# One ring of 4 KB buffers for a decoder trunk's weights, late FFN features, q and k and pooled features, and each quad's first product placed ahead of the preceding quad's last

## The chip, the cores and the metric

The kernel runs on one core of a Trainium2 chip. The metric is the device time of one execution in microseconds (us); lower is better.

## The reference, cut to what matters

```python
D_MODEL, SEQ, DEPTH, D_FF = 1024, 512, 2, 2816      # float32 throughout

def swiglu(x, w_gu, w_down):
    g, u = jnp.split(x @ w_gu, 2, axis=-1)
    return (jax.nn.silu(g) * u) @ w_down

for i in range(DEPTH):                              # mixer 0: attention, 1: pooling
    x = layer_norm(ALPHA * x + 0.5 * swiglu(x, ffn_w_gu[i, 0], ffn_w_down[i, 0]), ...)
    x = layer_norm(ALPHA * x + mixer_i(x), ...)
    x = layer_norm(ALPHA * x + 0.5 * swiglu(x, ffn_w_gu[i, 1], ffn_w_down[i, 1]), ...)
```

Six stages follow one another on 512 tokens of 1024 channels: FFN, attention (8 heads, T5 bias), FFN, FFN, pooling mixer (four groups with a causal mean each), FFN. Each ends in a LayerNorm, and the next stage needs its result.

## The kernel before, in words

**Phases.** The profile's span divides into FFN 0 (0 to 363 us), attention (363 to 588), FFN 2 (588 to 932), FFN 3 (932 to 1278), pooling (1278 to 1382) and FFN 5 (1382 to 1736).

**Precision.** Every float32 operand is split in two (`split`, L94): ScalarE copies it to fp32r (L96, `hi`), VectorE subtracts that from it (L97, `lo`). A product is three matmuls (`mm3`, L101 to L103).

**Weights.** They stream from memory in pieces of 512 KB (4 KB in each partition). SyncE issues the loads (L183), in the order in which the pieces are used; where a sum of two pieces is wanted, GpSimd adds the second by an accumulating DMA (L185). The pieces lie in a ring `raw` of 7 buffers. A weight *unit* is a piece, or a sum of pieces made by two adds on VectorE (`Quad.sums`, L139), split to `hi` and `lo`, each in a ring of 5. `run_ahead` keeps 5 units split ahead of TensorE, called from `retire` whenever a unit has been used; `load_ahead` loads a piece once the piece seven before it has been used up.

**FFN.** The first block has four plain units, done for the first half of the tokens (`h=0`) and then for the second (`h=1`). The second half's first operand, x8, is what `Seven.put` splits from the last token tiles. Between the halves, `x.sums()` forms the sums of x that the quads need (`form`, L279, then a split). Then come ten *quads*: Strassen's scheme with seven products, in the order 1, 2, 6, 5, 7, 3, 4, each one unit of 24 matmuls of 256 columns. Products are kept by ScalarE (L504) or added by VectorE (`ca`, `cb`, L507); the gate writes the FFN's features to `hT` (L512), 22 blocks of 2 KB. Products 1, 6, 7 and 4 accumulate one after the other in one bank; `cb` reads it after product 7, so product 4 waits for that add. After that come the down projection, residual and LayerNorm (L344 to L367), and transposes to feature-major order (L312, then L323 on ScalarE or L321 on VectorE), of which the last token tiles' come in the next phase.

**Order.** TensorE's order is that of the program. VectorE, ScalarE, GpSimd and SyncE run what a scheduler set at build time, in order on each engine. Buffers with one tag are given out as they are free.

Of the kernel before, what the change touches and what calls it, by code (L numbers as in the profile page):

```python
# [79 lines left out]
def trunk(ctx, tc, x, rel_bias, ln_g, ln_b, w_gu, w_dq, w_down, a_in, a_out, b_in, b_group, b_scale, b_out, onehot, out):  # L80
# [67 lines left out]

    def ffn_units(l, m):
        for i in range(4):  # L150
            plain(w_gu[l, m, 0, i])
        for jj in QUADS:
            q = Quad(w_gu[l, m, jj])
            for i in LATER:
                q.unit(i)
        both = [Quad(w_dq[l, m, q]) for q in range(2)]
        pieces[-10:] = [q.pieces[i] for group in ((0,), (1,), (2,), (3,), (4,)) for q in both for i in group]
        for i in LATER:
            for q in both:
                q.unit(i)  # L160
        b_plain(w_down[l, m], range(BLOCK, NF))
# [25 lines left out]

    def load_ahead():
        while len(loaded) < len(pieces) and (len(loaded) < RAW or pieces[len(loaded) - RAW].uses == 0):
            load()  # L190

    def prepare():
# [3 lines left out]
        hi = wp.tile([P, 1024], F32R, tag="hi", bufs=PARTS, name=f"hi{i}")  # L196
        lo = wp.tile([P, 1024], F32R, tag="lo", bufs=PARTS, name=f"lo{i}")
# [275 lines left out]
    def bias_rows(room):  # L473

        oh, gs, rb = room[0:BUCKETS, 0:GW], room[0:H, 1024:1024 + GW], room[0:BUCKETS, 2048:2048 + H]
        nc.gpsimd.dma_start(oh, onehot)
        nc.gpsimd.dma_start(rb, rel_bias)
        gp = bank(6, "gp")
        nc.tensor.matmul(gp[:H, :], rb, oh[:, 0:512], start=True, stop=True)
# [14 lines left out]
    def ffn(n, x, dest):  # L494
        with tc.tile_pool(name=f"ffn{n}", bufs=1) as fp:
            hT = fp.tile([P, NF, S], F32, name=f"hT{n}")
            kept = {}
# [50 lines left out]
            for jj in QUADS:  # L548
                if n == 0 and jj == 2:
# [1 line left out]
                if n == 0 and jj == 4:
                    bias_rows(hT[:, 14:22, :].rearrange("p f c -> p (f c)"))
                if jj == 2:
# [1 line left out]
                ca = fp.tile([P, 2, S], F32, tag="ca", name=f"ca{n}_{jj}")
                cb = fp.tile([P, 2, 256], F32, tag="cb", name=f"cb{n}_{jj}")
                banks = [bank(i, f"gu{n}_{jj}_{i}") for i in (2 * ((jj + 1) % 3), 2 * ((jj + 1) % 3) + 1, 6 + jj % 2)]
                for i in LATER:
                    acc = banks[BANKS[i]]
                    for _ in product([acc[:, 0:256], acc[:, 256:512]], weights(), x.parts[i], i in (1, 2, 5), i in (2, 3, 4)):  # L560
                        pass
                    if i in (1, 6):
                        keep(i, jj, acc, 2)
                    elif i == 5:
                        keep(i, jj, acc, 1)
                    elif i == 2:
                        add(ca[:, :, 0:256], acc, 1, jj)
                    elif i == 3:
                        add(ca[:, :, 256:512], acc, 6, jj)
                        ins = gate(2 * jj, 0, 512, ca[:, 0, :], ca[:, 1, :], 1.0)  # L570
                        if 3 <= jj < 3 + NT:
                            update_residual(ins)
                    elif i == 7:
                        add(cb, acc, 5, jj)
                        gate(2 * jj + 1, 256, 512, cb[:, 0, :], cb[:, 1, :], -1.0)
                    else:
                        gate(2 * jj + 1, 0, 256, acc[:, 0:256], acc[:, 256:512], -1.0)
                    retire()
                    if jj == QUADS[-1] and i in (2, 6, 3):
                        next(operands)  # L580
# [43 lines left out]
    def attention(n, x, dest):  # L624
        with tc.tile_pool(name="att", bufs=1) as ap:
            oT, qk, v, probs, pT = {}, {}, {}, {}, {}

            def project(acc, nm, h):
                two = [ap.tile([P, S], F32R, tag=f"{nm}{i}", bufs=2, name=f"{nm}{i}_{h}") for i in range(2)]
                split(two[0], two[1], acc)  # L630
                qk[nm, h] = two
# [111 lines left out]
    def pooling(n, x, dest):  # L743
        with tc.tile_pool(name="pool", bufs=1) as pp:
# [7 lines left out]
            def pool(acc, cc):  # L752
# [131 lines left out]
```

## Time and profile before

| | |
|---|---|
| runs | 1738.93 us median of 3 (1737.85 to 1741.2) |
| profiled execution | 1737.85 us, span 1736.1 us |
| TensorE | 1705.0 us busy (98%), mean granted clock 0.997 |
| VectorE | 1251.3 us (72%) |
| ScalarE | 825.6 us (48%) |
| GpSimd | 94.5 us (5%) |
| DMA | 257.30 MB, mean 148 GB/s |
| chain that ended last | TensorE 93%, DMA 3%, VectorE 2%, issue 1% |

The busy figures are shares of the whole span. A matmul's end is modelled and matmuls overlap, so the space between matmuls is read from their starts. A wait at one place need not show in the shares; it shows in the list of waits and in windows of time.

### The profile page before, as it was taken

What the parts mean: (1) busy time and instruction counts of PE and PEld (TensorE: products, weight loads), DVE (VectorE), ACT (ScalarE), POOL (GpSimd) and SP (SyncE); (2) the same over time, 40 slices, a digit from 0 to 9 for tenths busy, and PEclk for the clock granted to TensorE, in tenths of its full rate; (3) what the DMA queues carried; (4) which work ended last, traced back from release to release, by engine and by line L of the source; (5) the groups of instructions that cost most, each with busy time, mean ns of one, the idle gap of its engine ahead of it and who ended that gap; (6) DMA issues with size and microseconds to landing.
All of it is one profiled execution on the core that took longest, in us unless ns stands there. A gap on an engine that the chain in (4) does not pass through costs nothing.

```text
span 1736.1 us, 28083 instructions
## 1 busy us (share of the span) xinstructions
PE 1705.0 (98%) x11555; PEld 1585.1 (91%) x11555; DVE 1251.3 (72%) x1657; ACT 825.6 (48%) x1161; POOL 94.5 (5%) x132
## 2 busy tenths in 40 slices
PE   7999999999999999999999999999999999999998
PEld 6999998889888899999888999998888899999886
DVE  5777698266665877878928778788279787877946
ACT  5545464254443555455525554564254454545620
POOL 1010000000000000000000000000000000000000
PEclk9999999999999999999999999999999999999999
DMA  6787756323221376666633666756223356776611
GB/s 209 188 238 186 189 146 209 97 74 110 86 86 51 109 194 176 185 181 164 194 97 85 183 182 185 184 154 197 96 88 106 99 166 187 185 189 180 185 62 49
DMA packets 84864, 257.30 MB, mean 148 GB/s; under 512 B 8128, under 2 KB 25576, under 8 KB 84736
## 3 DMA queue, kind: packets, MB, share of 16 engines
q1 hardware_dynamic: 70080, 202.40, 35.0%
q0 software_dynamic: 14656, 53.12, 17.1%
q8 instruction: 90, 1.47, 0.3%
q14 instruction: 38, 0.31, 0.1%
HBM read 253.37 MB, written 4.74 MB: 149 GB/s over the span
## 4 chain that ended last, share of the span: by engine, by line
PE 93%; DMA 3%; DVE 2%; issue 1%; ACT 0%; SPq 0%; DVEq 0%; POOLq 0%
PE gu L101 16%; PE gu L102 16%; PE gu L103 16%; PE acc L102 8%; PE acc L103 8%; PE acc L101 8%; DMA raw<-in_ffn_w_gu 2%; PE qk L103 2%; PE da L102 2%; PE da L101 2%; PE da L103 2%; PE qk L101 2%; PE qk L102 2%; PE d L102 1%; PE d L103 1%; PE d L101 1%
## 5 line engine op out<-in xcount | busy, mean ns | idle before, releaser
L96 ACT ACTIVATE hi<-raw 128x1024 fp32r<-128x1024 f32 x458 | 484.6, 1061 | 661.4 <-PE gu L102 251.8
L97 DVE TENSOR_TENSOR lo<-raw,hi 128x1024 fp32r<-128x1024 f32 x458 | 557.5, 1222 | 323.6 <-ACT hi L96 322.0
L101 PE MATMUL gu<-x,hi 128*128 128x256 f32 x2496 | 710.3, 285 | 12.4 <-DVE x L97 6.7
L102 PE MATMUL gu<-x,hi 128*128 128x256 f32 x2496 | 707.8, 284 | 0.0
L103 PE MATMUL gu<-x,lo 128*128 128x256 f32 x2496 | 707.7, 284 | 0.0
L101 PEld LDWEIGHTS gu<-x,hi 128*128 128x128 f32 x2496 | 480.7, 193 | 16.6 <-DVE x L97 9.7
L102 PEld LDWEIGHTS gu<-x,hi 128*128 128x128 f32 x2496 | 480.8, 193 | 0.0
L103 PEld LDWEIGHTS gu<-x,lo 128*128 128x128 f32 x2496 | 480.6, 193 | 0.0
L101 PE MATMUL acc<-lo,h 128*128 128x512 f32 x448 | 174.8, 390 | 0.0
L103 PE MATMUL acc<-hi,h 128*128 128x512 f32 x448 | 174.3, 389 | 0.0
L102 PE MATMUL acc<-hi,h 128*128 128x512 f32 x448 | 174.3, 389 | 0.0
L139 DVE TENSOR_TENSOR raw<-raw,raw 128x1024 f32<-128x1024 f32 x96 | 117.5, 1224 | 22.6 <-DMA raw<-in_ffn_w_gu 20.3
L185 POOL DMA_DIRECT2D raw<-in_ffn_w_gu x80 | 69.3, 866 | 1070.0 <-DMA raw<-in_ffn_w_gu 736.4
L103 PEld LDWEIGHTS acc<-hi,h 128*128 128x128 f32 x448 | 84.1, 188 | 17.5
L101 PEld LDWEIGHTS acc<-lo,h 128*128 128x128 f32 x448 | 84.1, 188 | 17.4
L102 PEld LDWEIGHTS acc<-hi,h 128*128 128x128 f32 x448 | 84.1, 188 | 17.1
L507 DVE TENSOR_TENSOR ca<-gu,kept 128x512 f32<-128x512 f32 x80 | 55.2, 691 | 32.3 <-PE gu L103 32.3
L504 ACT ACTIVATE kept<-gu 128x512 f32<-128x512 f32 x120 | 69.5, 580 | 0.0
L323 ACT ACTIVATE st<-tp,cols 128x128 f32<-128x128 f32 x140 | 53.0, 466 | 20.2 <-PE tp L312 20.2
L97 DVE TENSOR_TENSOR x<-st,x 128x512 fp32r<-128x512 f32 (+1 forms) x64 | 51.4, 820 | 15.4 <-ACT x L96 14.8
L101 PE MATMUL qk<-x,hi 128*128 128x512 f32 (+1 forms) x160 | 56.4, 353 | 1.1 <-ACT hi L96 1.0
L103 PE MATMUL qk<-x,lo 128*128 128x512 f32 (+1 forms) x160 | 55.6, 347 | 1.2 <-DVE sm L352 1.2
(155 smaller groups left out, 2101.1 us busy)
## 6 DMA issues: line engine op xcount, KB each, us to landing
raw<-in_ffn_w_gu SPq DMA_DIRECT2D x216, 512.0 KB, 5.8
raw<-in_ffn_w_gu POOLq DMA_DIRECT2D x80, 512.0 KB, 8.3
raw<-in_ffn_w_down SPq DMA_DIRECT2D x56, 512.0 KB, 4.2
raw<-in_ffn_w_dq SPq DMA_DIRECT2D x40, 512.0 KB, 4.0
raw<-in_a_w_in SPq DMA_DIRECT2D x24, 512.0 KB, 3.6
raw<-in_ffn_w_dq POOLq DMA_DIRECT2D x16, 512.0 KB, 5.7
raw<-in_a_w_out SPq DMA_DIRECT2D x8, 512.0 KB, 3.8
raw<-in_b_w_in SPq DMA_DIRECT2D x8, 512.0 KB, 3.5
```

The lines of the kernel that those rows point to most:

```text
L96: nc.scalar.activation(hi, src, AF.Copy)
L97: return nc.vector.tensor_tensor(lo, src, hi.bitcast(F32), op=ALU.subtract)
L101: nc.tensor.matmul(acc, sh, ml, start=first, stop=False, skip_group_check=shared)
L102: nc.tensor.matmul(acc, sh, mh, start=False, stop=False, skip_group_check=shared)
L103: nc.tensor.matmul(acc, sl, mh, start=False, stop=last, skip_group_check=shared)
L139: nc.vector.tensor_tensor(d, d, more, op=ALU.add)
L185: nc.gpsimd.dma_start(p.tile, p.plus, accum_op=ALU.add)
L323: nc.scalar.activation(src[:, i, :], tp[:, c], AF.Identity, scale=g, bias=b)
L504: nc.scalar.activation(kept[i, jj], acc, AF.Copy)
L507: nc.vector.tensor_tensor(out, two(acc), two(kept.pop((i, jj))), op=ALU.add)
```

## The change

1. **One ring.** Pieces, `hi` and `lo` take buffers of one tag, 24 of 4 KB (before: 7 + 5 + 5). The FFN's features from block 8 on move there as well (`hT` shrinks from 22 blocks to 8, by 28 KB), and so do q and k in attention, the pooled features in pooling, and the one-hot of the bias.
2. **More ahead where the ring has room.** `held` counts buffers that the features (or q and k, or pooled features) take. With none held, nine pieces may be in use and seven units be split ahead; with the ring full, 7 and 5 as before. Attention holds 4, pooling 6, an FFN 1 from its third quad, growing to 7 by its ninth. A load is asked for by the count of pieces still in use, not by the seventh piece before it.
3. **Order of products.** `ORDER` puts product 1 of each quad ahead of product 4 of the quad before.
4. **Head.** In FFN 0 the splits and sums that follow the first block's units are placed behind the last split of x (`issue_after`). The one-hot is loaded in the second quad, not at the start.

The instructions are the same in number and kind on every engine; lines move down by one to 29. L94 to L103 become L95 to L104, L139 L140, L279 L284, L507 L525, L512 L530, L367 L372.

```diff
+SLOTS = 24
+    ORDER = [(1, 1)] + [(i, jj + (i == 1)) for jj in QUADS for i in (2, 6, 5, 7, 3, 1, 4) if (i, jj) != (1, QUADS[-1])]
     def ffn_units(l, m):
         ...
-        for jj in QUADS:
-            q = Quad(w_gu[l, m, jj])
-            for i in LATER:
-                q.unit(i)
+        gu = {jj: Quad(w_gu[l, m, jj]) for jj in QUADS}
+        for i, jj in ORDER:
+            gu[jj].unit(i)
     def load():
-        p.tile = wp.tile([P, 1024], F32, tag="raw", bufs=RAW, name=f"raw{len(loaded)}")
+        p.tile = wp.tile([P, 1024], F32, tag="slot", bufs=SLOTS, name=f"raw{len(loaded)}")
+    def free():
+        return SLOTS - RAW - 2 * PARTS - held[0]
     def load_ahead():
-        while len(loaded) < len(pieces) and (len(loaded) < RAW or pieces[len(loaded) - RAW].uses == 0):
+        while len(loaded) < len(pieces) and sum(p.uses > 0 for p in loaded[-32:]) < RAW + 2 * (free() > 1):
             load()
     def prepare():
-        hi = wp.tile([P, 1024], F32R, tag="hi", bufs=PARTS, name=f"hi{i}")
-        lo = wp.tile([P, 1024], F32R, tag="lo", bufs=PARTS, name=f"lo{i}")
+        hi = wp.tile([P, 1024], F32R, tag="slot", bufs=SLOTS, name=f"hi{i}")
+        lo = wp.tile([P, 1024], F32R, tag="slot", bufs=SLOTS, name=f"lo{i}")
     def run_ahead():
-        while len(parts) < min(len(units), retired[0] + PARTS):
+        while len(parts) < min(len(units), retired[0] + PARTS + max(0, free() - 2) // 2):
         def put(self, t, half, src):
-            split(o[:, 0, :, c], o[:, 1, :, c], src)
+            self.last = split(o[:, 0, :, c], o[:, 1, :, c], src)
     def ffn(n, x, dest):
-            hT = fp.tile([P, NF, S], F32, name=f"hT{n}")
+            hT = fp.tile([P, BLOCK, S], F32, name=f"hT{n}")
+            def room(jj):
+                if 2 * jj >= BLOCK:
+                    later[jj] = wp.tile([P, 2, S], F32, tag="slot", bufs=SLOTS, name=f"hT{n}_{jj}")
+                held[0] = max(0, min(jj + 2, NF // 2) - BLOCK // 2)
-                        retire()
+                        with tc.issue_after(x.last.ins) if n == 0 else ExitStack():
+                            retire()
-            for jj in QUADS:
+            for i, jj in ORDER:
...
     def attention(n, x, dest):
+        held[0] = 4
...
-                two = [ap.tile([P, S], F32R, tag=f"{nm}{i}", bufs=2, name=f"{nm}{i}_{h}") for i in range(2)]
+                two = wp.tile([P, 2, S], F32R, tag="slot", bufs=SLOTS, name=f"{nm}{h}")
     def pooling(n, x, dest):
+        held[0] = 6
...
-                    pT[g] = [pp.tile([P, 2, S], F32R, tag=f"pT{i}_{g % 3}", name=f"pT{i}_{g}") for i in range(2)]
+                    pT[g] = [wp.tile([P, 2, S], F32R, tag="slot", bufs=SLOTS, name=f"pT{i}_{g}") for i in range(2)]
```

**Where instructions move.** In the rows below a tile's name is followed by its number; `raw`, `hi` and `lo` belong to weights, `st` is x before its split, x0_8 is FFN 0's operand 8.

VectorE at the head, before:

```order
L97 TENSOR_TENSOR lo3_148<-raw3_95,hi3_147 128x1024
L97 TENSOR_TENSOR lo4_285<-raw4_268,hi4_284 128x1024
L97 TENSOR_TENSOR x0_8_203<-st0_0_1_201,x0_8_203 128x4x128
L97 TENSOR_TENSOR x0_3_213<-st0_1_1_211,x0_3_213 128x4x128
L139 TENSOR_TENSOR raw4_268<-raw4_268,raw6_272 128x1024
L279 SCALAR_TENSOR_TENSOR st0_0_0_104<-st0_0_0_104,st0_0_1_201 128x1024
L97 TENSOR_TENSOR x0_8_203<-st0_0_1_201,x0_8_203 128x4x128
L97 TENSOR_TENSOR x0_3_213<-st0_1_1_211,x0_3_213 128x4x128
L279 SCALAR_TENSOR_TENSOR st0_0_1_201<-st0_0_1_201,st0_1_1_211 128x1024
L97 TENSOR_TENSOR x0_5_313<-st0_0_0_104,x0_5_313 128x1024
```

and with the change:

```order
L98 TENSOR_TENSOR lo3_148<-raw3_95,hi3_147 128x1024
L98 TENSOR_TENSOR x0_8_203<-st0_0_1_201,x0_8_203 128x4x128
L98 TENSOR_TENSOR x0_3_213<-st0_1_1_211,x0_3_213 128x4x128
L284 SCALAR_TENSOR_TENSOR st0_0_0_104<-st0_0_0_104,st0_0_1_201 128x1024
L98 TENSOR_TENSOR x0_8_203<-st0_0_1_201,x0_8_203 128x4x128
L98 TENSOR_TENSOR x0_3_213<-st0_1_1_211,x0_3_213 128x4x128
L284 SCALAR_TENSOR_TENSOR st0_0_1_201<-st0_0_1_201,st0_1_1_211 128x1024
L98 TENSOR_TENSOR x0_5_331<-st0_0_0_104,x0_5_331 128x1024
L284 SCALAR_TENSOR_TENSOR st0_0_0_104<-st0_0_0_104,st0_1_1_211 128x1024
L284 SCALAR_TENSOR_TENSOR st0_1_0_126<-st0_0_0_104,st0_1_0_126 128x1024
L98 TENSOR_TENSOR x0_6_335<-st0_0_0_104,x0_6_335 128x1024
L98 TENSOR_TENSOR lo4_291<-raw4_268,hi4_290 128x1024
```

The split lo4 and the first L139 (now L140) stood ahead of the form and of x8's second split; lo4 now stands behind six forms and splits of x, and the sum further back.

VectorE in FFN 3's start, from the normalization of token tile 2 on (L367, now L372), before:

```order
L367 TENSOR_SCALAR ax_74<-ax_74,sm2_2_9286 128x512 x2
L97 TENSOR_TENSOR x3_1_9311<-st3_0_0_9306,x3_1_9311 128x4x128
L344 SCALAR_TENSOR_TENSOR ax_74<-acc2_3_1_8880,ax_74 128x512
L345 BN_STATS st2_3_9350<-ax_74 128x6
L97 TENSOR_TENSOR lo237_9412<-raw189_9008,hi237_9411 128x1024
L97 TENSOR_TENSOR x3_2_9324<-st3_1_0_9319,x3_2_9324 128x4x128
L351 BN_AGGR sm2_3_9351<-st2_3_9350 128x2
L97 TENSOR_TENSOR lo238_9418<-raw190_9041,hi238_9417 128x1024
L352 TENSOR_SCALAR sm2_3_9351<-sm2_3_9351 128x1
L97 TENSOR_TENSOR lo239_9424<-raw191_9071,hi239_9423 128x1024
L357 RECIPROCAL sm2_3_9351<-sm2_3_9351 128x1
L97 TENSOR_TENSOR lo240_9430<-raw192_9104,hi240_9429 128x1024
```

and with the change, from the instruction behind the same small one (L360, now L365):

```order
L98 TENSOR_TENSOR lo239_9429<-raw191_9012,hi239_9428 128x1024
L372 TENSOR_SCALAR ax_74<-ax_74,sm2_2_9296 128x512 x2
L98 TENSOR_TENSOR x3_1_9321<-st3_0_0_9316,x3_1_9321 128x4x128
L349 SCALAR_TENSOR_TENSOR ax_74<-acc2_3_1_8880,ax_74 128x512
L98 TENSOR_TENSOR lo240_9436<-raw192_9045,hi240_9435 128x1024
L98 TENSOR_TENSOR x3_2_9334<-st3_1_0_9329,x3_2_9334 128x4x128
L350 BN_STATS st2_3_9360<-ax_74 128x6
L98 TENSOR_TENSOR lo241_9440<-raw193_9075,hi241_9439 128x1024
L356 BN_AGGR sm2_3_9361<-st2_3_9360 128x2
L140 TENSOR_TENSOR raw192_9045<-raw192_9045,raw194_9108 128x1024
L357 TENSOR_SCALAR sm2_3_9361<-sm2_3_9361 128x1
L140 TENSOR_TENSOR raw193_9075<-raw193_9075,raw192_9045 128x1024
```

A split (lo239) stands in front of the normalization. The units are two further on: lo237 and lo238 were split in the phase before. Both sums of the first quad stand in these rows; before, the first comes two rows further down and the second while the first block's second half runs. After these rows come lo242, then tile 3's normalization, then the first split of x8, which was ahead of that normalization.

VectorE from the first to the second quad of FFN 3, before:

```order
L97 TENSOR_TENSOR lo247_9825<-raw197_9421,hi247_9824 128x1024
L139 TENSOR_TENSOR raw197_9421<-raw197_9421,raw199_9663 128x1024
L97 TENSOR_TENSOR lo248_9855<-raw198_9427,hi248_9854 128x1024
L139 TENSOR_TENSOR raw198_9427<-raw198_9427,raw197_9421 128x1024
L507 TENSOR_TENSOR cb3_1_9726<-gu3_1_4_9727,kept3_1_5_9852 128x512
L97 TENSOR_TENSOR lo249_9889<-raw197_9421,hi249_9888 128x1024
```

and with the change, where lo246 is the second quad's first product and lo247 the first quad's last:

```order
L98 TENSOR_TENSOR lo246_9742<-raw197_9179,hi246_9741 128x1024
L98 TENSOR_TENSOR lo247_9774<-raw196_9146,hi247_9773 128x1024
L140 TENSOR_TENSOR raw197_9179<-raw197_9179,raw199_9425 128x1024
L98 TENSOR_TENSOR lo248_9809<-raw198_9209,hi248_9808 128x1024
L525 TENSOR_TENSOR ca3_1_9780<-gu3_1_5_9746,kept3_1_1_9771 128x2x256
L140 TENSOR_TENSOR raw198_9209<-raw198_9209,raw197_9179 128x1024
L98 TENSOR_TENSOR lo249_9841<-raw197_9179,hi249_9840 128x1024
L98 TENSOR_TENSOR lo250_9873<-raw199_9425,hi250_9872 128x1024
L98 TENSOR_TENSOR lo251_9907<-raw200_9432,hi251_9906 128x1024
L525 TENSOR_TENSOR cb3_1_9781<-gu3_1_4_9745,kept3_1_5_9870 128x512
```

The first sum of the second quad (raw197) still stands ahead of cb3_1, with more work between them. Product 4 waits for cb3_1 as before; the unit ahead of it on TensorE was product 3, and is now lo246, in another bank.

## Rows read from the trace of the kernel before

**Rows 1.** The page's first part: busy time, share of the span and instructions of each engine.

```profile
PE 1705.0 (98%) x11555; PEld 1585.1 (91%) x11555; DVE 1251.3 (72%) x1657; ACT 825.6 (48%) x1161; POOL 94.5 (5%) x132
```

**Rows 2.** TensorE's waits, of the whole span: what waited, for which engine's tile and line; us in total, times, longest.

```profile
PE gu L101 <- DVE x L97: 6.7, 4, 5.7
PE gu L101 <- DVE cb L507: 5.4, 3, 2.8
PE qk L103 <- DVE sm L352: 1.2, 1, 1.2
PE u L103 <- DVE lo L97: 1.1, 1, 1.1
PE qk L101 <- ACT hi L96: 1.0, 1, 1.0
```

**Rows 3.** Windows of 40 us: for each engine the busy us and the instructions, then the granted clock as a share of full speed, the DMA engines' share and GB/s.

```profile
0.00:40.00 40.00, 27.43 (x185) 26.74 (x186) 21.43 (x23) 20.21 (x27) 5.20 (x13) 0.91 0.68 227
1000.00:1040.00 40.00, 40.00 (x336) 40.00 (x335) 30.25 (x33) 20.09 (x26) 3.46 (x4) 1.00 0.68 182
```

**Rows 4.** TensorE's timeline at the head: start, us, engine, line, operation, tiles, count; in brackets the idle time before and what ended it.

```profile
25.49 0.28 PE L103 MATMUL gu<-x,lo 128*128 128x256 f32 x1
31.45 0.58 PE L101 MATMUL gu<-x,hi 128*128 128x256 f32 x1 [5.67 <-DVE x L97]
...
35.03 0.34 PE L102 MATMUL gu<-x,hi 128*128 128x256 f32 x1
35.21 0.28 PE L103 MATMUL gu<-x,lo 128*128 128x256 f32 x1
```

**Rows 5.** VectorE's timeline at the head, same columns.

```profile
16.08 3.78 DVE L97 TENSOR_TENSOR lo<-raw,hi 128x1024 fp32r<-128x1024 f32 x3 [1.48 <-ACT hi L96]
20.12 1.29 DVE L97 TENSOR_TENSOR x<-st,x 128x512 fp32r<-128x512 f32 x2 [0.26 <-ACT x L96]
28.43 1.23 DVE L139 TENSOR_TENSOR raw<-raw,raw 128x1024 f32<-128x1024 f32 x1 [7.01 <-DMA raw<-in_ffn_w_gu]
29.57 1.22 DVE L279 SCALAR_TENSOR_TENSOR st<-st,st 128x1024 f32<-128x1024 f32 x1
30.71 1.29 DVE L97 TENSOR_TENSOR x<-st,x 128x512 fp32r<-128x512 f32 x2
```

**Rows 6.** Windows of 5 us, columns as in rows 3: after the wait at the head, and the two that hold the waits of 1.86 and 2.76 us.

```profile
30.00:35.00 5.00, 3.55 (x16) 3.56 (x17) 4.96 (x6) 1.06 (x1) 0.00 (x0) 0.50 0.00 1
975.00:980.00 5.00, 3.14 (x26) 2.94 (x26) 4.97 (x7) 2.45 (x4) 0.00 (x0) 1.00 0.10 20
1425.00:1430.00 5.00, 2.24 (x19) 2.04 (x18) 4.97 (x6) 2.35 (x3) 0.00 (x0) 1.00 0.06 11
```

**Rows 7.** TensorE's timeline in attention's start.

```profile
366.49 0.39 PE L101 MATMUL qk<-x,hi 128*128 128x256 f32 x1 [1.04 <-ACT hi L96]
...
368.19 0.39 PE L103 MATMUL qk<-x,lo 128*128 128x256 f32 x1 [1.19 <-DVE sm L352]
```

**Rows 8.** TensorE's timeline where the first quad of the second, third and fourth FFN begins its product 4.

```profile
632.07 0.39 PE L101 MATMUL gu<-x,hi 128*128 128x256 f32 x1 [0.81 <-DVE cb L507]
...
977.80 0.39 PE L101 MATMUL gu<-x,hi 128*128 128x256 f32 x1 [1.86 <-DVE cb L507]
...
1428.73 0.39 PE L101 MATMUL gu<-x,hi 128*128 128x256 f32 x1 [2.76 <-DVE cb L507]
```

**Rows 9.** VectorE's timeline around the second of these.

```profile
973.52 1.23 DVE L139 TENSOR_TENSOR raw<-raw,raw 128x1024 f32<-128x1024 f32 x1 [3.94 <-DMA raw<-in_ffn_w_gu]
...
975.92 1.22 DVE L139 TENSOR_TENSOR raw<-raw,raw 128x1024 f32<-128x1024 f32 x1
977.06 0.68 DVE L507 TENSOR_TENSOR cb<-gu,kept 128x512 f32<-128x512 f32 x1
```

**Rows 10.** ScalarE's timeline at the head.

```profile
22.51 1.09 ACT L315 ACTIVATE st<-tp 128x512 f32<-128x512 f32 x2 [1.90 <-PE tp L312]
23.48 1.15 ACT L96 ACTIVATE x<-st 128x512 fp32r<-128x512 f32 x2
```

**Rows 11.** TensorE's timeline where the third FFN's first block begins its second half.

```profile
946.89 0.38 PE L101 MATMUL gu<-x,hi 128*128 128x256 f32 x1 [0.33 <-DVE x L97]
```

**Rows 12.** VectorE's timeline in the third FFN's start.

```profile
930.84 1.00 DVE L367 TENSOR_SCALAR ax<-ax,sm 128x512 f32<-128x512 f32 x2
...
939.53 1.22 DVE L139 TENSOR_TENSOR raw<-raw,raw 128x1024 f32<-128x1024 f32 x1
...
941.52 1.00 DVE L367 TENSOR_SCALAR ax<-ax,sm 128x512 f32<-128x512 f32 x2
...
943.73 1.37 DVE L321 TENSOR_SCALAR st<-tp,cols 128x128 f32<-128x128 f32 x4 [0.61 <-PE tp L312]
...
946.15 2.43 DVE L97 TENSOR_TENSOR x<-st,x 128x512 fp32r<-128x512 f32 x3
```

**Rows 13.** The page's sixth part: DMA issues by tile and issuing queue, count, KB each, median us from issue to landing.

```profile
raw<-in_ffn_w_gu SPq DMA_DIRECT2D x216, 512.0 KB, 5.8
raw<-in_ffn_w_gu POOLq DMA_DIRECT2D x80, 512.0 KB, 8.3
```

**Rows 14.** SyncE's waits, of the whole span, columns as in rows 2.

```profile
SPq L183 <- DVE lo L97: 1035.4, 283, 25.1
```

**Rows 15.** The page's fifth part: the group of weight splits on VectorE (count, busy us, mean ns of one, idle before, and what ended most of it).

```profile
L97 DVE TENSOR_TENSOR lo<-raw,hi 128x1024 fp32r<-128x1024 f32 x458 | 557.5, 1222 | 323.6 <-ACT hi L96 322.0
```

More of the change, by code (lines that the diff above doesn't have):

```diff
@@ L471, in trunk, with bias_load, bias_rows @@
     gr = dram.tile([H, P, GW], F32, name="gr")
[L473 to L477, printed above, removed]
+    def bias_load():
+        oh = wp.tile([BUCKETS, GW + H], F32, tag="slot", bufs=SLOTS, name="oh")
+        gs = wp.tile([H, GW], F32, tag="slot", bufs=SLOTS, name="gs")
+        nc.gpsimd.dma_start(oh[:, 0:GW], onehot)
+        nc.gpsimd.dma_start(oh[:, GW:], rel_bias)
+        return oh, gs
+    def bias_rows(oh, gs):
         gp = bank(6, "gp")
-        nc.tensor.matmul(gp[:H, :], rb, oh[:, 0:512], start=True, stop=True)
+        nc.tensor.matmul(gp[:H, :], oh[:, GW:], oh[:, 0:512], start=True, stop=True)
         nc.vector.tensor_copy(gs[:, 0:512], gp[:H, :])
@@ L546, in ffn @@
                                  lambda: fp.tile([P, 4, 256], F32, tag="ca", name=f"u2{n}"))
[L548 to L549 removed]
+            quads = {}
+            for i, jj in ORDER:
+                if n == 0 and (i, jj) == (1, 2):
                     columns()
[L551 to L553 removed]
+                    onehots = bias_load()
+                if n == 0 and (i, jj) == (1, 4):
+                    bias_rows(*onehots)
+                if (i, jj) == (1, 2):
@@ L554, in ffn @@
                     load_residual()
[L555 to L580, printed above, removed]
@@ new lines, in ffn @@
+                if i == 1:
+                    quads[jj] = [bank(b, f"gu{n}_{jj}_{b}") for b in (2 * ((jj + 1) % 3), 2 * ((jj + 1) % 3) + 1)]
+                if i == 2:
+                    room(jj)
+                    ca = fp.tile([P, 2, S], F32, tag="ca", name=f"ca{n}_{jj}")
+                    cb = fp.tile([P, 2, 256], F32, tag="cb", name=f"cb{n}_{jj}")
+                    quads[jj].append(bank(6 + jj % 2, f"gu{n}_{jj}_{6 + jj % 2}"))
+                acc = quads[jj][BANKS[i]]
+                for _ in product([acc[:, 0:256], acc[:, 256:512]], weights(), x.parts[i], i in (1, 2, 5), i in (2, 3, 4)):
+                    pass
@@ new lines, in ffn @@
+                if i in (1, 6):
+                    keep(i, jj, acc, 2)
+                elif i == 5:
+                    keep(i, jj, acc, 1)
+                elif i == 2:
+                    add(ca[:, :, 0:256], acc, 1, jj)
+                elif i == 3:
+                    add(ca[:, :, 256:512], acc, 6, jj)
+                    ins = gate(2 * jj, 0, 512, ca[:, 0, :], ca[:, 1, :], 1.0)
+                    if 3 <= jj < 3 + NT:
+                        update_residual(ins)
+                elif i == 7:
+                    add(cb, acc, 5, jj)
+                    gate(2 * jj + 1, 256, 512, cb[:, 0, :], cb[:, 1, :], -1.0)
+                else:
+                    gate(2 * jj + 1, 0, 256, acc[:, 0:256], acc[:, 256:512], -1.0)
@@ L584, in ffn @@
+                retire()
+                if jj == QUADS[-1] and i in (2, 6, 3):
+                    next(operands)
             accs = {0: (bank(0, f"da{n}_0"), bank(1, f"da{n}_1"))}
@@ L611, in act @@
                     two = glob.tile([P, 2, 2, S], F32R, tag="act", bufs=ACT, name=f"h{n}_{f // 2}")
-                    split(two[:, 0], two[:, 1], hT[:, f // 2 * 2:f // 2 * 2 + 2, :])
+                    split(two[:, 0], two[:, 1], later[f // 2])
+                    held[0] -= 1
                     pairs[f // 2] = two
```

14 lines of the change are left out of this document (9 added, 5 removed).

## The prediction

> **What bounds the kernel now.** I read the summary first: TensorE is busy 1705.0 of 1736.1 us [rows 1], so what can be won is its holes. The sum below is made against the profiled execution, 1737.85 us, of which 1736.1 are span; the median of the runs is 1738.93, 1.08 more, and I add that at the end. Second, TensorE's waits [rows 2]: 6.7 us for splits of x, 5.4 for the add called cb, and three waits of 1.0 to 1.2 near the starts of phases. Third, the windows [rows 3]: the first 40 us hold only 27.43 us of matmuls, while 1000 to 1040 is full: 336 matmuls, 0.12 us each, 2.88 us for a weight unit of 24. In that full window VectorE is busy 30.25 of 40 us. So inside the quads a change has nothing to win; it wins or loses at the head, at the five phase starts and at the first quad of each FFN. The timelines then say what each hole waits for.
>
> At the head TensorE stops 5.67 us [rows 4] for a split of x. VectorE, whose instructions run in the order written, had stood 7.01 us before a sum of two weight pieces (L139) whose second piece was still landing; the L279 and the x split stood behind it [rows 5]. The granted clock is 0.50 in 30:35, the 1.2 GHz level [rows 6]. From 31.45 to 35.21 the 17 matmuls took 3.76 us instead of 17 x 0.12 = 2.04, so the clock cost 1.7.
>
> In attention's start TensorE waits 1.04 and 1.19 us [rows 7] for splits of weights that VectorE and ScalarE do only after the LayerNorm tail; in pooling's start 1.1 [rows 2]. In the last three FFNs TensorE waits 0.81, 1.86 and 2.76 us [rows 8] before product 4 of the first quad: cb stands behind L139, and L139 behind a landing (3.94 us idle in one of them) [rows 9].
>
> **The change, part by part.** The bracketed idle counts from the modelled end of the matmul before; from start to start each wait is some 0.17 longer (25.49 to 31.45 is 5.96, less the 0.12 pace is 5.84). I use +0.17 for all seven waits.
>
> (a) *First quad's splits behind x's at the head.* lo4 and the first L139 leave their place ahead of L279. L279 needs the transposed tile that ScalarE starts writing at 22.51 and ends the first half of by about 23.1 (half of 1.09); x's second cast starts at 23.48 [rows 10]. L279 then runs 23.1 to 24.3 (1.22) and the split 24.3 to 25.0 (0.69), 0.6 before TensorE is free at 25.61. The wait goes and the low clock with it: **-5.84 - 1.72 = -7.6**. What comes late next is lo4: four more L279 and x splits and one x6 stand before it, by 1.2 each from 25.6 to about 32.7. TensorE needs it after four units, 25.6 + 4 x 2.88 = 37.1. The sum L139 comes at about 35, past the 28.43 at which its piece had landed [rows 5], and lo6, at 39.9, is needed at 42.9. Covered.
>
> (b) *Up to seven units split ahead at a phase's end.* For attention and pooling the late splits now stand before the LayerNorm tail, so the waits of 1.04 + 1.19 + 1.1 + 3 x 0.17 = 3.8 go. But one split now stands between the tail's last small instruction and its normalization, and VectorE has no idle time there: 1.22 less the 0.08 by which neighbours overlap, and 0.2 of slack, is 0.95 later at both starts. Net **-3.8 + 1.9 = -1.9**.
>
> (c) *The same at the three FFN starts.* Here the wait to be won is small (0.33 [rows 11]), and two things come forward: one lo before tile 2's normalization, and a second L139 before tile 3's, since the first quad is split two units earlier. VectorE is gapless from 930.84 to 942.5; the 0.61 before L321 is a wait for TensorE [rows 12] and moves along. From row to row I get +1.14 for the second sum, less 0.6 as one x split moves from before the normalization to after it, plus 0.6 as another moves behind L321: x8's second split ends 948.0 instead of 946.83. If ScalarE's casts in front of it shift too, 948.6. So +1.2 to +1.75 at each, I take 1.4: **3 x 1.4 = +4.2**. TensorE's first half starts about 1.1 later and waits a little more at the second; that is inside the 1.4, not beside it. From both sides: nothing if ScalarE is what ends last anyway; 2 x 1.22 = 2.44 if both moved operations count in full.
>
> On the clock: the waits of 1.86 and 2.76 were not followed by a low clock; it is 1.00 in the windows that hold them [rows 6], and only the 5.67 at the head was. The Trainium skill, TensorE: Matmul & The Clock Gate, section "HAM oscillation — how this bites in real kernels", says otherwise in its example: an engine that waits between pieces of work starts each next piece at half clock. By the rows a start that is 1.4 later costs 1.4; by that rule it would cost the clock as well, which is a rival below.
>
> (d) *First quad to second.* Two covers are laid over one wait. Loads run nine ahead and the pieces of the second quad are asked for while the down projection still runs, some 30 us before they are summed, against a landing of 8.3 us for the accumulated ones [rows 13]. And product 1 of the second quad, 2.88 us, now stands between products 7 and 4. Each alone exceeds 2.76 + 0.17. So **-(0.81 + 1.86 + 2.76 + 0.5) = -5.9**, and 0.1 for each slower restart, **-6.2**.
>
> (e) *The rest.* Features, q and k, pooled features and the one-hot change their place in memory, with the same instructions: 0. The gates that now write into the ring wait, in the program, for the same work as before. Two more pieces at the head are 1 MB on the queues after raw6's: what they could delay is the landing at 28.43, and L139 has moved to 35: 0.
>
> Sum: -7.6 - 1.9 + 4.2 - 6.2 = -11.5; **I take -11**, since (a) has only 0.6 to spare. That is 1726.9 for an execution like the profiled one, and **1727.9** against the median.
>
> **The rivals.**
> *Early splits cost nothing* (0.15). If the splits at the starts fill time in which VectorE would have waited, +4.2 and +1.9 vanish and the three waits of 0.33 may go: 1738.93 - 7.6 - 3.8 - 6.2 - 0.7 = 1720.6. Against it: VectorE shows no gap there [rows 12].
> *The head does not come through* (0.12). If L279 waits for more of the tile than I think, or something of x is late, TensorE still waits, and enough to lose the clock again: 1727.9 + 3 to 7 = 1731 to 1735. For it: the margin of 0.6.
> *The clock falls at the starts* (0.04), by the rule above. Five starts at 1.7 would be 8.5: 1736.4. Against it: the 1.00 after 2.76.
> *Slower: the common ring makes SyncE late* (0.08). Today a piece's slot is freed by a split (283 waits for lo, [rows 14]); in the common ring it may take a slot that the last matmul of a unit frees, and every later load stands behind that wait on SyncE's queue. A load then lands 5.8 us after its issue, an accumulated one 8.3 more [rows 13], and the split (1.22 [rows 15]) after that. If in each of the 4 x 10 quads one unit came late by x, the loss is 40 x: it eats the 11 us at x = 0.28 and is slower at over 0.36. With x = 0.5: 1747.9. Against it: when features fill the ring, seven pieces and five units are left, as before, and loads are asked for no later in the order written.
> *Nothing of the kind* (0.04): gains of (a) and (d) given back unit by unit, about 1737. Here also falls a ring that holds fewer free slots than meant.
>
> **How the numbers follow.** My case has 0.57, by its bounds 1723 to 1731: the starts at 0.4 to 2.44 each, the margin of (a). The range is to leave out 0.2: it takes in most of the first rival and of the second, **1720.5 to 1734.5**. 0.2% is 3.5 us, about what a measurement of this kernel tells from no change: faster is below 1735.5, slower above 1742.4. Faster: 0.57 + 0.15 + 0.12 and half of the clock's case, **0.86**; same, the rest of the clock's, nothing, and the ring's mild part, **0.08**; slower **0.06**.
>
> **What would show it.** Right: no TensorE wait above 1 us before 40 us and a clock of 1.00 in 30:35; cb gone from the list of TensorE's waits; in the last three FFNs the first x8 matmul 1.1 to 1.8 us later after the phase's last down matmul; the windows in mid-FFN still full. Wrong: L139 still ahead of L279 in time; TensorE waits for lo in mid-FFN or for a piece in a down projection; starts that are not later, or later by more than 2.4; the PEclk row under 1.00 at a start.

## The result: 1726.91 us against 1738.84, and the profile after

The median of six runs is **1726.91 us** (1726.37 to 1729.08); that of the kernel before, run beside it, is 1738.84 (1737.85 to 1741.2, six runs). The ratio is 0.993 (95% interval 0.9918 to 0.9943), 11.9 us less. 1727.9 had been forecast, within 1720.5 to 1734.5. The profiled execution took 1726.37 us, its span 1724.2, against 1737.85 and 1736.1.

Summary of the changed kernel (against [rows 1]): the same instructions, and a TensorE that is busy 1701.4 of 1724.2 us, so 22.8 us of holes are left of 31.1.

```profile
PE 1701.4 (99%) x11555; PEld 1582.5 (92%) x11555; DVE 1240.8 (72%) x1657; ACT 824.8 (48%) x1161; POOL 93.8 (5%) x132
```

TensorE's waits, all that the view lists (against [rows 2]): us in total, times, longest.

```profile
PE tp L317 <- DMA ax<-in_x: 6.7, 2, 3.6
PE gu L102 <- DVE x L98: 5.3, 6, 1.0
PE qk L102 <- DVE x L98: 0.8, 1, 0.8
PE u L102 <- DVE x L98: 0.8, 1, 0.8
PE s L102 <- DVE pr L690: 0.7, 3, 0.2
```

The waits for cb and for lo are gone from the list, and so is the one long wait for x. One stop that the view leaves out is new, 0.2 us in the last quad of FFN 3 (from 1149.50 to 1149.84 in place of 0.12), where VectorE's cb at 1149.10 stands behind a sum that waits for a landing:

```profile
1147.96 1.23 DVE L140 TENSOR_TENSOR raw<-raw,raw 128x1024 f32<-128x1024 f32 x1 [2.03 <-DMA raw<-in_ffn_w_dq]
```

What is left after the first loads of x are six waits of 0.8 to 1.0 for x (three FFN starts, twice each), the two starts of the mixers at 0.8, and three small new ones in attention's scores (`pr` is what VectorE makes of a row of them). The windows (columns as in [rows 3]) show the head, its stretch that had the clock at 0.50 [rows 6], and mid-FFN:

```profile
0.00:40.00 40.00, 33.33 (x255) 32.80 (x256) 26.56 (x27) 25.44 (x33) 5.93 (x13) 1.00 0.96 316
30.00:35.00 5.00, 5.00 (x44) 5.00 (x43) 5.00 (x5) 4.97 (x6) 1.01 (x2) 1.00 1.04 269
1000.00:1040.00 40.00, 40.00 (x336) 40.00 (x335) 30.03 (x34) 19.27 (x25) 3.42 (x4) 1.00 0.67 167
```

Where the time went, from the starts of the same matmuls in the two profiled executions:

| place | forecast | measured |
|---|---|---|
| first loads, up to 25.49 before | 0 | -0.8 |
| head, wait and low clock (a) | -7.6 | -7.4 |
| attention's start (b) | -1.6 | -2.0 |
| attention, the scores | 0 | +1.6 |
| three FFN starts, up to the second half of the first block (c) | +4.2 | 3 x 1.05 = +3.2 |
| first to second quad (d) | -6.2 | -1.07 - 2.11 - 3.01 = -6.2 |
| last quad of FFN 3 | 0 | +0.3 |
| pooling's start (b) | -0.3 | -0.5 |
| sum | -11.5, taken as -11 | -11.9 |

The head on VectorE (against [rows 5]):

```profile
18.25 1.29 DVE L98 TENSOR_TENSOR x<-st,x 128x512 fp32r<-128x512 f32 x2 [0.26 <-ACT x L97]
22.34 1.23 DVE L284 SCALAR_TENSOR_TENSOR st<-st,st 128x1024 f32<-128x1024 f32 x1 [2.79 <-ACT st L320]
23.49 1.28 DVE L98 TENSOR_TENSOR x<-st,x 128x512 fp32r<-128x512 f32 x2
...
34.02 1.22 DVE L140 TENSOR_TENSOR raw<-raw,raw 128x1024 f32<-128x1024 f32 x1
```

The form (L284) starts when its tile is there, at 22.34, x's split follows, and the sum L140 comes at 34.02 without a wait. It is there earlier than worked out (22.34 and not 23.1) because TensorE, which transposes x, was 0.8 earlier by then, the -0.8 of the table. Of this 0.2 stands in front of the first matmul of a weight; the other 0.6 comes by 14.7 us, for those matmuls start 0.21 us apart, as at the clock of 0.50 in [rows 6], until 13.1 us with the change and until 14.7 before. That the clock's rise comes at another time is not an effect that the change was shown to have (e7).

FFN 3's start, TensorE's two waits (the second against [rows 11]):

```profile
924.84 0.39 PE L102 MATMUL gu<-x,hi 128*128 128x256 f32 x1 [0.80 <-DVE x L98]
...
939.28 0.39 PE L102 MATMUL gu<-x,hi 128*128 128x256 f32 x1 [0.95 <-DVE x L98]
```

and VectorE in the same place (against [rows 12]):

```profile
921.99 0.14 DVE L365 TENSOR_TENSOR sm<-sm 128x1 f32<-128x1 f32 x1
922.05 1.22 DVE L98 TENSOR_TENSOR lo<-raw,hi 128x1024 fp32r<-128x1024 f32 x1
923.19 1.00 DVE L372 TENSOR_SCALAR ax<-ax,sm 128x512 f32<-128x512 f32 x2
...
928.89 1.17 DVE L140 TENSOR_TENSOR raw<-raw,raw 128x1024 f32<-128x1024 f32 x1
...
930.10 1.22 DVE L140 TENSOR_TENSOR raw<-raw,raw 128x1024 f32<-128x1024 f32 x1
...
933.28 1.00 DVE L372 TENSOR_SCALAR ax<-ax,sm 128x512 f32<-128x512 f32 x2
...
938.54 2.43 DVE L98 TENSOR_TENSOR x<-st,x 128x512 fp32r<-128x512 f32 x3
```

Between the small instruction at 921.99 and the normalization at 923.19 stands a split of 1.22, and both sums stand before the last tile's normalization at 933.28. The first normalization began 0.19 behind its small instruction before, 1.20 now. From the last down matmul to the end of x8's second split (0.68 into the row at 938.54) it is now 15.6 us, and was 14.5: +1.05.

The first quad's end in FFN 3, VectorE (against [rows 9]): cb follows a split, and no sum with a landing to wait for. The piece for which the sum had waited (raw199) is now asked for in the down projection of FFN 2: GpSimd's add to it is issued at 904.57 and has landed at 910.20, 45 us before the sum at 955.06. Before, it was issued at 963.84 and landed at 973.43. GpSimd, before and now:

```profile
963.84 0.86 POOL L185 DMA_DIRECT2D raw<-in_ffn_w_gu  x1 [44.43 <-DVE lo L97]
```

```profile
904.57 0.85 POOL L187 DMA_DIRECT2D raw<-in_ffn_w_gu  x1 [18.97 <-DMA raw<-in_ffn_w_gu]
```

VectorE with the change:

```profile
965.44 1.23 DVE L98 TENSOR_TENSOR lo<-raw,hi 128x1024 fp32r<-128x1024 f32 x1 [1.64 <-PE gu L103]
966.58 0.68 DVE L525 TENSOR_TENSOR cb<-gu,kept 128x512 f32<-128x512 f32 x1
```

SyncE's waits (against [rows 14]). Its loads now mostly wait for matmuls, as the slower rival had it (607.0 us for the matmuls of gu alone), and TensorE's mid-FFN window is still full: 336 matmuls in 40 us.

```profile
SPq L185 <- PE gu L104: 607.0, 143, 18.0
SPq L185 <- DVE lo L98: 203.7, 66, 5.6
```

### The profile page after: what moved, and what is told of

Its sections match the earlier page's. It is cut to its first block, busy times and chain, and to the rows that moved or that the text cites. A ratio compares the mean times of both kernels' runs of the same rounds, so it can differ in the third digit from the quotient of the medians.

```text
span 1724.2 us, 27993 instructions
## 1 busy us (share of the span) xinstructions
PE 1701.4 (99%) x11555; PEld 1582.5 (92%) x11555; DVE 1240.8 (72%) x1657; ACT 824.8 (48%) x1161; POOL 93.8 (5%) x132
## 4 chain that ended last, share of the span: by engine, by line
PE 94%; DVE 4%; DMA 1%; issue 1%; ACT 0%; SPq 0%; DVEq 0%; POOLq 0%
PE gu L102 17%; PE gu L103 17%; PE gu L104 17%; PE acc L102 7%; PE acc L104 7%; PE acc L103 7%; PE qk L102 2%; PE qk L103 2%; PE qk L104 2%; PE da L102 2%; PE da L103 2%; PE da L104 2%; PE d L102 1%; PE d L103 1%; PE d L104 1%; DVE lo L98 1%
## 5 line engine op out<-in xcount | busy, mean ns | idle before, releaser
L103 PE MATMUL gu<-x,hi 128*128 128x256 f32 x2496 | 706.8, 283 | 0.0
L104 PE MATMUL gu<-x,lo 128*128 128x256 f32 x2496 | 706.8, 283 | 0.0
L97 ACT ACTIVATE hi<-raw 128x1024 fp32r<-128x1024 f32 x458 | 479.2, 1056 | 369.0 <-DVE lo L98 252.4
L103 PEld LDWEIGHTS gu<-x,hi 128*128 128x128 f32 x2496 | 479.7, 192 | 0.0
L104 PEld LDWEIGHTS gu<-x,lo 128*128 128x128 f32 x2496 | 479.6, 192 | 0.0
L104 PE MATMUL acc<-hi,h 128*128 128x512 f32 x448 | 174.3, 389 | 0.0
L103 PE MATMUL acc<-hi,h 128*128 128x512 f32 x448 | 174.3, 389 | 0.0
L140 DVE TENSOR_TENSOR raw<-raw,raw 128x1024 f32<-128x1024 f32 x96 | 117.1, 1220 | 8.6 <-DMA raw<-in_ffn_w_dq 7.2
L104 PEld LDWEIGHTS acc<-hi,h 128*128 128x128 f32 x448 | 84.1, 188 | 17.6
L103 PEld LDWEIGHTS acc<-hi,h 128*128 128x128 f32 x448 | 84.1, 188 | 17.2
L525 DVE TENSOR_TENSOR cb<-gu,kept 128x512 f32<-128x512 f32 x40 | 27.6, 689 | 67.7 <-PE gu L104 67.7
L349 DVE SCALAR_TENSOR_TENSOR ax<-acc,ax 128x512 f32<-128x512 f32 x48 | 33.0, 688 | 55.7 <-PE acc L104 55.3
L529 ACT ACTIVATE sg<-cb 128x256 f32<-128x256 f32 x40 | 16.5, 412 | 94.5 <-DVE cb L525 94.5
```

What stands on the lines that cost most here:

```text
L97: nc.scalar.activation(hi, src, AF.Copy)
L103: nc.tensor.matmul(acc, sh, mh, start=False, stop=False, skip_group_check=shared)
L104: nc.tensor.matmul(acc, sl, mh, start=False, stop=last, skip_group_check=shared)
L140: nc.vector.tensor_tensor(d, d, more, op=ALU.add)
L349: nc.vector.scalar_tensor_tensor(r, y, self.scale, r, op0=ALU.mult, op1=ALU.add)
L525: nc.vector.tensor_tensor(out, two(acc), two(kept.pop((i, jj))), op=ALU.add)
```

## The experiments

Times are medians of runs interleaved with the kernel before, whose median was 1738.42 beside e1 to e4 and 1740.51 beside e5 to e8; ratios are to it, with their 95% interval. Single waits for cb are given from start to start of the matmuls, some 0.17 us more than the list has.

**e1, the head's order alone.** The kernel before with:

```diff
-                        retire()
+                        with tc.issue_after(x.last.ins) if n == 0 else ExitStack():
+                            retire()
```

> The kernel before with one thing changed: in FFN 0 the splits and sums behind the first block's units are placed behind x's last split on VectorE (lo4 stays ahead, the first sum L139 moves behind). Theory (the head's 7.6 us come from that order alone): the wait of 5.67 us and the half clock behind it go, nothing else moves: 1738.8 - 7.6 = 1731.2, TensorE's waits for cb still 5.4 us. Rival (the ring's earlier loads are needed as well): a wait of 2 us or more comes back for the first quad's lo before 60 us: 1733 or more.

1734.15 us, 0.9974 (0.9963 to 0.9985). TensorE's waits for cb, and windows (columns as in rows 3):

```profile
PE gu L101 <- DVE cb L507: 5.4, 4, 2.1
```

```profile
30.00:35.00 5.00, 5.00 (x44) 5.00 (x43) 5.00 (x6) 4.60 (x5) 0.00 (x0) 1.00 0.01 3
360.00:365.00 5.00, 3.81 (x19) 3.70 (x19) 4.89 (x12) 1.54 (x3) 0.00 (x0) 0.66 0.71 222
1420.00:1425.00 5.00, 2.90 (x16) 2.70 (x15) 4.97 (x7) 2.45 (x4) 0.00 (x0) 0.78 0.13 16
```

The long wait and the low clock at the head are gone: across them TensorE gains 7.6 us, as forecast. 3.2 us are lost again later, so the theory has the head but not the total; the rival has the total, but not the wait of 2 us for lo on which it was built. What is lost: a new wait of 0.74 for the first quad's cb at 54 us (against it, the other first quads wait 0.6 less in all), and the clock, which fell behind the two waits at attention's start (0.66) and behind the wait of 2.1 us at 1422: 1.5 us each. Waits like these stand in the kernel before too, and there as well the clock fell behind them in one execution (e9); that e1 made it likelier is not excluded.

In the full change the line `issue_after` does nothing: built without it, the program has the same rows in the same order on all five engines. With the common ring the scheduler puts lo4 and the sum behind x by itself.

**e2, the old rings.** The change with

```diff
-tag="slot", bufs=SLOTS, name=f"raw{len(loaded)}"    (and hi, lo)
+tag="raw", bufs=RAW, name=f"raw{len(loaded)}"       (hi, lo: bufs=PARTS)
-... < RAW + 2 * (free() > 1):
+... < RAW:
-... retired[0] + PARTS + max(0, free() - 2) // 2):
+... retired[0] + PARTS):
```

> The change with its ring undone: pieces, hi and lo again in rings of 7, 5 and 5, no more loaded or split ahead than before; the order of products, the head's order, the later one-hot and the features' move into buffers of 4 KB stay. Theory (the early splits cost at the starts, the product order alone covers the quads' waits of 0.97, 2.0 and 2.9): head as with the change, starts and attention as before, quads at 0 to 0.1: 1726.9 - 3 x 1.2 (FFN starts) + 1.5 (attention's and pooling's early splits lost) = about 1724.8, faster than the full change. Rival (the quads' gain is the ring's): the cb waits return in part, 1 to 6 us more than that: 1726 to 1731.

1742.14 us, 1.0017 (1.0006 to 1.0029): slower than before. The starts and attention were as before, as expected, and cb no longer waits at the first quads (the order of products covers it). But cb waits at the *last* quad of each FFN, 1.8, 2.2, 2.9 and 3.2 us. VectorE at the second of these:

```profile
804.25 1.23 DVE L140 TENSOR_TENSOR raw<-raw,raw 128x1024 f32<-128x1024 f32 x1 [2.20 <-DMA raw<-in_ffn_w_dq]
...
807.87 1.23 DVE L140 TENSOR_TENSOR raw<-raw,raw 128x1024 f32<-128x1024 f32 x1 [1.26 <-DMA raw<-in_ffn_w_dq]
809.01 0.68 DVE L525 TENSOR_TENSOR cb<-gu,kept 128x512 f32<-128x512 f32 x1
```

Both sums now belong to the down projection, and both wait for a landing, with cb behind them. Neither theory had this. The clock fell behind the last two of these waits and at attention's start as well, and the twelve runs lie far apart (1735.61 to 1746.64).

**e3, the old product order in the new ring.**

```diff
-    ORDER = [(1, 1)] + [(i, jj + (i == 1)) for jj in QUADS for i in (2, 6, 5, 7, 3, 1, 4) if (i, jj) != (1, QUADS[-1])]
+    ORDER = [(i, jj) for jj in QUADS for i in LATER]
```

> The change with the order of products as before (1, 2, 6, 5, 7, 3, 4 quad by quad); ring and all else stay. Theory (each cover of the quads' wait is enough alone): no wait for cb over 0.3 us, 1726.9 within 0.7. Rival (product 1 in between is needed): waits for cb of 1 to 3 us in three FFNs, 1728 to 1733.

1726.3 us, 0.9926 (0.9914 to 0.9939), the time of the full change. The waits for cb:

```profile
PE gu L102 <- DVE cb L525: 0.5, 2, 0.3
```

The ring alone takes the first quads' waits away; the two that the list shows stand at last quads (0.35 us at 236, 0.17 at 1150). The product order adds nothing measurable to it. In e4 below, with five units split ahead, the first quads' waits are gone too and the load of raw199 is issued as early (900.18 us, the change 900.52); in the old rings of e8 it is issued at 953.69, and the waits stay. So the loads are what counts; whether it is the nine in use or the common buffers that lets them go early was not tried apart.

**e4, five units ahead.**

```diff
-        while len(parts) < min(len(units), retired[0] + PARTS + max(0, free() - 2) // 2):
+        while len(parts) < min(len(units), retired[0] + PARTS):
```

> The change with five units split ahead at all times; the ring of 24 and nine loads stay. If the number of units ahead is what puts a split in front of the normalization at the starts, as the prediction has it: starts as before, 1726.9 - 3.6 + 1.5 = 1724.8. Rival (it is enough that hi and lo no longer have rings of their own, whose slots came free only at the tail; VectorE's order of this kernel still has that split there): starts as with the change, TensorE's first wait 0.96 and 1.0 or more at x8, 1726.9 within 0.7.

1732.35 us, 0.996 (0.9949 to 0.9972): a miss for both. The starts are as with the change, so the rival is right about them: the split gets in front of the normalization because its buffer is free, not because seven units are split ahead. The 5.4 us over the change came from elsewhere, pooling. TensorE's waits, and one window:

```profile
PE gu L102 <- DVE x L98: 5.2, 6, 1.0
PE u L102 <- ACT hi L97: 3.0, 1, 3.0
```

```profile
1300.00:1305.00 5.00, 4.50 (x10) 3.11 (x11) 5.00 (x8) 3.55 (x5) 0.00 (x0) 0.50 0.35 105
```

There a weight is not split in time (3.0 us), and the clock is at half behind it. With the change seven units are split when pooling begins, and its features then leave room for five: the two more carry it over this place. Why five are too few here, and were enough in the kernel before, stays open.

**e5, the starts cleared.** The change with

```diff
 tail = [self.take(f) for f in range(self.count - self.r, self.count)]
+run_ahead()
 ...
-retire(self.r)
+held[0], pending[0] = 1, self.r
 # ffn, first block, behind x.sums():
+with tc.issue_after(x.last.ins):
+    retire(pending[0])
 # attention and pooling: retire(pending[0]) behind the first halves of the projections
 # eight units ahead in the tail, with seven pieces loaded
```

> The change with the splits of the five phase starts taken out of the LayerNorm tail: the first four units of the next phase are split before the tail (eight ahead there, with seven pieces loaded), and the tail's own four units are counted as used only after the next phase has split its x (in an FFN behind x8 and x3). Theory (those splits are the 0.96 at each start and the 1.11 at x8): TensorE's waits at the starts fall to 0.2, at x8 to 0.5 or less: 5 x 0.8 + 3 x 0.6 to 1.1 = 5.8 to 7.3 less, about 1720. Rival (the tail's own small instructions and ScalarE set the start): starts stay at 0.9 to 1.0 and 1726.5 stands.

1720.64 us, 0.9893 (0.9876 to 0.9909), 6.3 less than the change and 6.4 less than e7 below, which is the change but for the one-hot and ran beside it. VectorE in FFN 3's start, and the waits that are left:

```profile
920.08 0.14 DVE L365 TENSOR_TENSOR sm<-sm 128x1 f32<-128x1 f32 x1
920.26 1.00 DVE L372 TENSOR_SCALAR ax<-ax,sm 128x512 f32<-128x512 f32 x2
...
925.36 1.01 DVE L372 TENSOR_SCALAR ax<-ax,sm 128x512 f32<-128x512 f32 x2
...
935.24 2.43 DVE L98 TENSOR_TENSOR x<-st,x 128x512 fp32r<-128x512 f32 x3
```

```profile
PE gu L102 <- DVE x L98: 1.0, 3, 0.3
PE s L102 <- DVE pr L697: 0.7, 3, 0.2
```

The normalization at 920.26 follows its small instruction at once and the last tile's comes 5.1 us later, not 10.1. The first matmuls of the phases wait 0.2, the x8 matmul 0.3 as before. So the splits in the tail were the starts' cost.

**e6, the scores cleared as well.**

```diff
-                retire(4)
+                retire(1)
                 vp = [weights(), weights()]
                 scores(h)
                 values(hp, vp, 0)
                 scores(h + 1)
+                retire(3)
```

> As e5, and in attention three of the four units that a head pair's projections use up are counted as used only behind the second head's scores, so that one split and not two stand between the rows of the scores on VectorE. Theory (the three waits of 0.34 for the scores' bank come from those splits): TensorE's waits for pr gone, another 1.0 to 1.4 less than e5: about 1719. Rival (the bank waits for softmax itself): the three waits stay, time as e5.

1719.62 us, 0.9887 (0.987 to 0.9903), the lowest median, 7.3 under the change. It is 1.0 under e5, and their runs overlap; the gain itself is read from the traces. TensorE's waits but for the first loads of x:

```profile
PE gu L102 <- DVE x L98: 1.0, 3, 0.3
PE gu L102 <- DVE cb L529: 0.2, 1, 0.2
```

The waits for pr are gone, and attention's middle is 1.55 us shorter than in e5 between the same two matmuls, the 1.6 of the table. VectorE at the same scores in the kernel before:

```profile
435.72 1.22 DVE L97 TENSOR_TENSOR lo<-raw,hi 128x1024 fp32r<-128x1024 f32 x1
...
439.48 0.68 DVE L664 SCALAR_TENSOR_TENSOR pr<-s,bias 128x512 f32<-128x512 f32 x1
```

and in the changed kernel, with the first of TensorE's three waits:

```profile
425.85 0.61 DVE L690 SCALAR_TENSOR_TENSOR pr<-s,bias 128x128 f32<-128x128 f32 x2
426.38 2.35 DVE L98 TENSOR_TENSOR lo<-raw,hi 128x1024 fp32r<-128x1024 f32 x2
...
429.17 1.22 DVE L98 TENSOR_TENSOR lo<-raw,hi 128x1024 fp32r<-128x1024 f32 x1
...
430.43 0.54 DVE L690 SCALAR_TENSOR_TENSOR pr<-s,bias 128x384 f32<-128x384 f32 x1
```

```profile
433.73 0.50 PE L102 MATMUL s<-k,q 128*128 128x512 f32 x1 [0.23 <-DVE pr L690]
```

The scores of a head have four rows; the entry at 425.85 is the first two. Three splits stand between the second and the third (430.43), and a fourth before the last, which ends at 433.67; the matmul at 433.73 needs its bank. Before, one split (435.72) stood among the four, and the last ended at 440.17, 3.3 us before the matmul that needs its bank (443.51).

**e7, the one-hot first.**

```diff
+            if n == 0:
+                onehots = bias_load()
             w = [weights() for _ in range(4)]
...
-                    onehots = bias_load()
```

> The change with the one-hot's two loads issued at the start again. Theory (the head's last 0.4 to 0.8, by which TensorE is earlier before any wait for VectorE, come from these loads' leaving the head's queues): 1727.0 to 1727.5, the first products 0.4 to 0.8 later, all else as with the change. Rival (that lead is chance in the arrival of x): 1726.6, no shift.

1727.01 us, 0.993 (0.9917 to 0.9943). The matmul at 25.49 is 0.9 later than with the change. But two further executions of the kernel before have it at 25.19 and 24.19 (e9, e10), and e3 to e6, with the loads as in the change, at 24.06 to 25.16. It varies by as much in either, so the 0.8 of the head's first stretch can be chance and is not settled.

**e8, old rings and old products.** e2 with e3's edit.

> e2 with the order of products as before: old ring sizes, the rule that counts pieces in use, the head's order. Theory (in the old rings it is the new product order that makes the last quad's cb wait for the down projection's pieces): no wait at the last quads, the first quads' 0.97, 2.0 and 2.9 back, 1738.4 - 7.6 - 0.6 = 1730 and up to 1.4 more for each wait that lowers the clock. Rival (the rule for loads makes it): waits of 1.8 to 3.2 at the last quads stay beside those of the first: 1740 or more.

1733.21 us, 0.9969 (0.9956 to 0.9982). The waits for cb:

```profile
PE gu L102 <- DVE cb L525: 6.3, 4, 3.0
```

They are at the first quads again, 1.7, 0.5, 1.6 and 3.1 (FFN 0's is new), and none is left at the last. The theory holds: in the old rings, product 1 ahead of product 4 moves the wait from the first quads to the down projection's pieces. The total is 3 over the 1730 of the waits that were expected: FFN 0's 1.7, and 1.4 to 1.5 of low clock behind each of two waits, against shorter waits at the other quads.

**e9 and e10, the kernel before again.**

> The kernel before, unchanged, for a second look at its clock. In e1, e2 and e8 the granted clock fell behind the two waits of 1.1 and 1.25 at attention's start (0.66 in one 5-us window, some 1.3 us lost); in the first profile of before it did not, behind the same waits. If that is a matter of one execution to the next, a further execution of before shows it or waits of 2 to 3 us at a first quad followed by a low clock, and a span up to 2 to 4 us longer than 1736.1. If it belongs to those kernels, the clock stays at 1.00 everywhere but at the head.

> As e9, a third look at the same kernel: a clock that falls behind the waits of 1.1 to 3 us in one execution and not in another, or a clock of 1.00 everywhere but at the head.

1739.53 and 1738.91 us. The windows of e9 at attention's start and behind the first quad of FFN 5:

```profile
365.00:370.00 5.00, 2.86 (x17) 2.66 (x18) 5.00 (x9) 2.88 (x4) 0.00 (x0) 0.87 0.52 146
370.00:375.00 5.00, 5.00 (x36) 5.00 (x36) 1.50 (x6) 2.48 (x7) 0.00 (x0) 0.79 1.03 354
1430.00:1435.00 5.00, 5.00 (x32) 5.00 (x31) 3.32 (x5) 2.23 (x4) 0.43 (x1) 0.66 0.65 197
```

At attention's start the waits are those of the first profile, 1.0 and 1.2 us; at FFN 5's first quad it is 2.2 us, where the first profile had 2.8. The clock falls behind both places, and the matmuls after each lose 1.5 us. In e10, with the same waits there as in e9, it falls only at FFN 5, in the first profile at neither place. In one and the same kernel it is a matter of the execution.

## Why the prediction was right, point by point

*(a) The head*: right in size, and e1 shows that the order of VectorE is enough for it. Wrong in the cause as the change states it: the line that was to bring the order changes nothing in the ring. The 0.6 of margin held (x8's split ended at about 24.2, half into the row at 23.49; TensorE was free at 24.82).

*(b) The mixers' starts*: the trade was as described, a wait for lo against a split of 1.22 ahead of the normalization. TensorE then waited 0.80 by the list, 0.96 from start to start, where 0.95 was taken; both starts gained a little more than forecast (-2.5 in all against -1.9).

*(c) The FFN starts*: a loss at a place that the change does not speak of, as forecast; 1.05 where 1.4 was taken. The row count gave 1.2 and ScalarE's casts, which were to add 0.55, added nothing. The words "up to seven units split ahead" and "split two units earlier" named the wrong cause: with five units the split and both sums stand at the same places (e4). What counts is that hi and lo no longer wait for buffers of their own, which came free at the tail's end. e5 gets all of it back.

*(d) The quads*: -6.2, to the tenth, and by the loads that were named: the piece was asked for in the down projection, 55 us before its sum where some 30 were taken. That each cover is enough was half right. The ring's is (e3). The product order's is enough at that place but makes a new wait at the last quad when the rings are small (e2, e8).

*(e) The rest, at nothing*: failed in attention, +1.6. I counted what the moved q and k wait for, not how far VectorE's splits shift among the scores' rows. e6 shows that it is those splits. The 0.3 at FFN 3's last quad, a sum in front of cb with a landing to wait for, was not foreseen either; it is there in e3 too, so it is not the product order's.

*The clock.* From 1.00 behind 1.86 and 2.76 I took it that such waits leave the clock alone. That was one execution: e9 and e10 show that it falls behind 1.0 plus 1.2 in one execution of three and behind 2.2 in two. The Trainium skill (TensorE: Matmul & The Clock Gate, section "HAM oscillation — how this bites in real kernels") has in its example a half clock behind every wait of about 3 to 5 us. The traces agree at the head, where the clock fell behind 5.67, 5.77 and 6.57 us (before, e9, e10); the waits elsewhere are shorter than the example's, and behind them it fell at times, so the 1.00 spoke less against that rival than I took it to. The waits of 0.8 to 1.0 that the change brings were followed by 1.00 in its profile. So some of the median's gain may be low clock that goes with the waits: the profiled execution of before, with none at these places, was 1.0 us under its median.

*The rivals.* The slower one saw the mechanism and not its price: SyncE does wait for matmuls, 607 us in 143 waits for those of gu, and the quads stay full; the one late landing that TensorE felt cost 0.3, and whether that wait made it late is not shown. In the first rival the three waits of 0.33 were put at 0.7; they are 1.0, which makes its time 1720.3. The chances and the range stand. That the forecast came within 1.0 us is in part luck: misses on one side (-0.8 at the first loads, which may be chance, -1.0 in (c), -0.6 in (b)) stand against +1.6 in attention and +0.3 at FFN 3's last quad.

## What to carry to other kernels

Freeing a buffer earlier moves every instruction that waited for it, also on an engine that runs in order, and there the place it moves to can be the end of a phase on which the next one waits; read the new order there first. Where a wait goes through an in-order engine, ask what stands in front of the last link (here a sum with a landing, then a split), and price each by its own row. Two covers of one wait are to be tried one by one: one can be idle, and in other surroundings harmful.

## What the runs showed of the hardware that was not expected

The granted clock behind a short stop of TensorE differs from one execution of the same program to the next. Behind waits of 1.0 and 1.2 us, whose ends are 1.7 us apart, it stayed at 1.00 in two of three executions of before and fell in one (0.87 and 0.79 in two windows of 5 us, 1.5 us lost); in e1, e2 and e8, with the same two waits, it fell in each. Behind 2.2 us at FFN 5's first quad it fell in two executions, behind 2.8 in the third it did not. The profiles without such waits (the change, e3, e5, e6, e7) show a mean of 0.999.
